# Kurtosis of long rows: the last stage in row form, whole rows for six groups, and dummy transposes before the last sums

## The chip, the cores and the metric

The kernel runs on one core of a Trainium2 chip. The metric is the device time of one execution in microseconds, and the median of several runs is compared. The engines named here are TensorE (PE in the profile, with PEld for its weight loads), VectorE (DVE), ScalarE (ACT), GpSimd (POOL) and SyncE (SP), which issues the DMAs.

## The reference

The input has 1024 rows of 8192 float32 values, 32 MB in all. For each row the excess kurtosis is wanted.

```python
mean = np.mean(x, axis=-1, keepdims=True)
std = np.std(x, axis=-1, keepdims=True)
z = (x - mean) / (std + 1e-8)
return (np.mean(z ** 4, axis=-1) - 3).astype(np.float32)
```

The kernels compute it as n * q / s^2 - 3, where s is the row's sum of squared deviations and q the sum of their squares, that is of the fourth powers.

## The kernel before, in words

**Tiling.** The rows are cut into 18 groups (`GROUPS`). A row is spread over k partitions, so that a group fills 128 partitions with 128/k rows, each partition holding 8192/k columns: k is 8 for the first two groups, 4 for the third and 2 for the other fifteen, which have 4096 columns in each partition. A group's entry gives k, the pieces of columns in which it is loaded (one DMA each), the number of columns whose fourth powers ScalarE takes, and the engine that forms the mean. There are five buffers of 4096 columns (`SLOT_OF`); a group's load is put on SP's queue when the group that held its buffer has been through its fourth powers.

**One group.** The mean comes first. For the early groups (`DVE`) VectorE adds the two halves of each partition with a sum (`added_halves`, L149), and a matmul with a block matrix adds the partitions of a row and divides (L159). For the later groups (`PE`) TensorE transposes the 32 blocks of 128 columns and adds them up in PSUM (`transposed_sums`, L132), VectorE adds the two partitions of a row (`pair_sums`, L138), and a matmul with a column sums up (L168). The last group has `both`: 28 blocks by TensorE and the last piece of 512 columns by VectorE (L164, L165). ScalarE copies the negative mean out of PSUM (`nmu`, L170). Then ScalarE squares the deviations in place, with their sum (`square`, L176). The fourth powers are squares of these: the first columns on ScalarE (L183), the rest on VectorE (L188), each with its sum.

**Order.** The order on each engine is the order of the program text, since the schedule is written out by hand. In step i of the loop stand the mean and the square of group i, the fourth powers of group i-1 on VectorE, the next loads, a piece of work of a finished batch, and the fourth powers of group i on ScalarE. So `pair_sums` of group i stands on VectorE before the fourth powers of group i-1.

**Batches.** The groups' sums are gathered in four batches, and `finish` works on a batch in three steps of the loop: `factor` adds the partitions' sums by a matmul (L204), and forms minus its reciprocal squared on VectorE (L206, L208); `scaled` adds the two engines' fourth powers and multiplies (L215, L216); `result` turns them to rows with a matmul (L226), subtracts 3 (L228), and issues the output DMA on SP (L230).

**The end.** The last group is squared in two halves (L273, L275). VectorE takes the fourth powers of the second half while ScalarE squares the first; then ScalarE takes 1664 columns of the first half and VectorE the other 384. The first-sum matmuls are three (L200 to L202). The last column gets a path of its own: ScalarE's part is scaled on ScalarE (`wa`, L282), VectorE's on VectorE (L284), and two matmuls add them (L226).

Of the kernel before, what the change touches and what calls it, by code (L numbers as in the profile page):

```python
# [7 lines left out]
f32 = mybir.dt.float32  # L8
bf16 = mybir.dt.bfloat16
AO = mybir.AluOpType  # L10
AF = mybir.ActivationFunctionType
P = 128
# [3 lines left out]
GROUPS = [  # L16
    (8, [1024], 0, 'DVE'),
    (8, [1024], 0, 'DVE'),
    (4, [2048], 0, 'DVE'),
    (2, [4096], 1280, 'DVE'),  # L20
    (2, [4096], 768, 'DVE'),
    (2, [4096], 1536, 'DVE'),
    (2, [2304, 1792], 640, 'PE'),
    (2, [2304, 1792], 640, 'PE'),
    (2, [2304, 1792], 640, 'PE'),
    (2, [2304, 1792], 640, 'PE'),
    (2, [2304, 1792], 640, 'PE'),
    (2, [2304, 1792], 640, 'PE'),
    (2, [2304, 1792], 640, 'PE'),
    (2, [1536, 1536, 1024], 512, 'PE'),  # L30
    (2, [1536, 1536, 1024], 512, 'PE'),
    (2, [1536, 1536, 1024], 512, 'PE'),
    (2, [1536, 1536, 1024], 512, 'PE'),
    (2, [1536, 1280, 768, 512], 1664, 'both'),
]

BATCHES = [[0, 1], [2], [3, 4, 5, 6, 7, 8, 9, 10, 11, 12], [13, 14, 15, 16, 17]]
SLOT_W = 4096
SLOT_OF = [0, 1, 2, 3, 0, 1, 2, 3, 4, 0, 1, 2, 3, 4, 0, 1, 2, 3]
HALVES = 2  # L40


@with_exitstack
def kernel(
# [5 lines left out]
    nc = tc.nc  # L50
    n_rows, n_cols = x.shape
# [3 lines left out]
    L = NG - 1  # L55
    KS = [g[0] for g in GROUPS]
# [4 lines left out]
    const = ctx.enter_context(tc.tile_pool(name="const", bufs=1))  # L61
    small = ctx.enter_context(tc.tile_pool(name="small", bufs=4))
    fin = ctx.enter_context(tc.tile_pool(name="fin", bufs=4))
    psum = ctx.enter_context(tc.tile_pool(name="psum", bufs=2, space=bass.MemoryType.PSUM))
    psfin = ctx.enter_context(tc.tile_pool(name="psfin", bufs=1, space=bass.MemoryType.PSUM))
    ctx.enter_context(tc.manual_schedule())

    zeros = const.tile([P, 512], f32, name="zeros")
# [4 lines left out]
    blk = {}  # L73

    def block_matrix(k):
        r = P // k
        b = const.tile([P, P], f32, name=f"blk{k}")
        v = b.rearrange("p (r k) -> p r k", k=k)
        nc.gpsimd.memset(b, neg_inv_n)
        nc.gpsimd.affine_select(  # L80
            out=v, in_=v, pattern=[[-k, r], [0, k]], base=0,
            channel_multiplier=1, compare_op=AO.is_ge, fill=0.0)
        nc.gpsimd.affine_select(  # L83
            out=v, in_=v, pattern=[[k, r], [0, k]], base=k - 1,
            channel_multiplier=-1, compare_op=AO.is_ge, fill=0.0)
        blk[k] = b

    for k in dict.fromkeys(k for k in KS if k > 2):
        block_matrix(k)
    ident = const.tile([P, P], f32, name="ident")  # L90
    nc.gpsimd.memset(ident, 1.0)
    nc.gpsimd.affine_select(
        out=ident, in_=ident, pattern=[[-1, P]], base=0,
        channel_multiplier=1, compare_op=AO.is_equal, fill=0.0)
    negcol = const.tile([P, 1], f32, name="negcol")
    nc.gpsimd.memset(negcol, neg_inv_n)
    block_matrix(2)
    junk = const.tile([P, 2048], bf16, name="junk")

    where = {}
    stats = []
    for b in BATCHES:
        n = len(b) + (b[-1] == L)
        s2, qa, qd = (const.tile([P, n], f32, name=f"{t}_{b[0]}") for t in ("s2", "qa", "qd"))
        if any(GROUPS[i][2] == 0 for i in b):
            nc.gpsimd.memset(qa, 0.0)
        stats.append((s2, qa, qd))
        for j, i in enumerate(b):  # L110
            where[i] = (j, s2, qa, qd)

    slots = [xpool.tile([P, SLOT_W], f32, name=f"xt{s}") for s in sorted(set(SLOT_OF))]
    xts = {}
    nmus = {}

    def load(i):
        k, pieces = GROUPS[i][:2]
        w = n_cols // k
        assert sum(pieces) == w  # L120
        xt = slots[SLOT_OF[i]]
        xts[i] = xt[:, :w]
        src = x[ROWS[i]:ROWS[i + 1], :].rearrange("r (k w) -> (r k) w", k=k)
        c = 0
        for w in pieces:
            nc.sync.dma_start(out=xt[:, c:c + w], in_=src[:, c:c + w])  # L126
            c += w
# [42 lines left out]
        nc.scalar.copy(nmu, mps)  # L170
        nmus[i] = nmu

    def square(i, c0=0, c1=None, extra=0):
        j, s2, qa, qd = where[i]
        t = xts[i][:, c0:c1]
        nc.scalar.activation(out=t, in_=t, func=AF.Square, bias=nmus[i],  # L176
                             accum_out=s2[:, j + extra:j + extra + 1])

    def fourth_act(i, c0, c1):
        j, s2, qa, qd = where[i]  # L180
        if c1 > c0:
            t = xts[i][:, c0:c1]
            nc.scalar.activation(out=t, in_=t, func=AF.Square, accum_out=qa[:, j:j + 1])  # L183

    def fourth_dve(i, c0, c1=None, extra=0):
        j, s2, qa, qd = where[i]
        t = xts[i][:, c0:c1]
        nc.vector.tensor_tensor_reduce(  # L188
            out=t, in0=t, in1=t, scale=1.0, scalar=0.0,
            op0=AO.mult, op1=AO.add, accum_out=qd[:, j + extra:j + extra + 1])  # L190

    def factor(b):
        s2 = stats[BATCHES.index(b)][0]
        n = len(b)
        k = KS[b[0]]
        p2 = psfin.tile([P, n], f32, name="p2")
        if b[-1] == L:
            nc.tensor.matmul(p2[:, :n - 1], lhsT=blk[k], rhs=s2[:, :n - 1], start=True, stop=True)  # L200
            nc.tensor.matmul(p2[:, n - 1:n], lhsT=blk[k], rhs=s2[:, n - 1:n], start=True, stop=False)  # L201
            nc.tensor.matmul(p2[:, n - 1:n], lhsT=blk[k], rhs=s2[:, n:n + 1], start=False, stop=True)  # L202
        else:
            nc.tensor.matmul(p2, lhsT=blk[k], rhs=s2, start=True, stop=True)  # L204
        rec = fin.tile([P, n], f32, name="rec")
        nc.vector.reciprocal(rec, p2)  # L206
        fac = fin.tile([P, n], f32, name="fac")
        nc.vector.scalar_tensor_tensor(  # L208
            out=fac, in0=rec, scalar=-1.0, in1=rec, op0=AO.mult, op1=AO.mult)
        return fac  # L210

    def scaled(b, fac, n):
        s2, qa, qd = stats[BATCHES.index(b)]
        w4 = fin.tile([P, len(b)], f32, name="w4")
        nc.vector.tensor_add(w4[:, :n], qa[:, :n], qd[:, :n])  # L215
        nc.vector.tensor_mul(w4[:, :n], w4[:, :n], fac[:, :n])  # L216
        return w4

    def result(b, terms):
        n = len(b)  # L220
        k = KS[b[0]]
        r = P // k
        sel = blk[k].rearrange("p (r k) -> p r k", k=k)[:, :, 0]
        pk = psfin.tile([n, r], f32, name="pk")
        for j, t in enumerate(terms):
            nc.tensor.matmul(pk, lhsT=t, rhs=sel, start=j == 0, stop=j == len(terms) - 1)  # L226
        kr = fin.tile([n, r], f32, name="kr")
        nc.vector.tensor_scalar_add(kr, pk, -3.0)  # L228
        dst = out[ROWS[b[0]]:ROWS[b[-1] + 1]].rearrange("(g r) -> g r", r=r)
        nc.sync.dma_start(out=dst, in_=kr)  # L230

    def finish(b):
        fac = factor(b)
        yield
        w4 = scaled(b, fac, len(b))
        yield
        result(b, [w4])


    held = {}  # L240
# [2 lines left out]
    def load_next(done):  # L243
        while to_load and held.get(SLOT_OF[to_load[0]], -1) <= done:
            i = to_load.pop(0)
            held[SLOT_OF[i]] = i
            load(i)

    load_next(-1)
    STEPS = [(7, 8, 9), (9, 10, 11), (13, 14, 15)]  # L250
    steps = {}
    for b, ats in zip(BATCHES[:-1], STEPS):
        f = finish(b)
        for at in ats:
            steps.setdefault(at, []).append(f)
    for i in range(L):
        mean(i)
        square(i)
        if i >= 1:
            fourth_dve(i - 1, GROUPS[i - 1][2])  # L260
            load_next(i - 1)
        for f in steps.get(i, ()):
            next(f, None)
        fourth_act(i, 0, GROUPS[i][2])


    k, _, a, _ = GROUPS[L]
    h = n_cols // k // 2
    b = BATCHES[-1]
    n = len(b)  # L270
    s2, qa, qd = stats[-1]
    mean(L)
    square(L, h, 2 * h)  # L273
    fourth_dve(L - 1, GROUPS[L - 1][2])
    square(L, 0, h, extra=1)  # L275
    fourth_dve(L, h, 2 * h)
    fourth_act(L, 0, a)
    fac = factor(b)
    w4 = scaled(b, fac, n - 1)
    wa = fin.tile([P, n], f32, name="wa")  # L280
    nc.gpsimd.memset(wa, 0.0)
    nc.scalar.activation(out=wa[:, n - 1:], in_=qa[:, n - 1:n], func=AF.Copy, scale=fac[:, n - 1:])  # L282
    fourth_dve(L, a, h, extra=1)
    nc.vector.scalar_tensor_tensor(  # L284
        out=w4[:, n - 1:], in0=qd[:, n:], scalar=qd[:, n - 1:n], in1=fac[:, n - 1:],
        op0=AO.add, op1=AO.mult)
    result(b, [wa, w4])


# [28 lines left out]
```

## Time and profile before

| what | value |
|---|---|
| median of five runs | 98.29 us (97.79 to 98.79) |
| the profiled execution's own time | 98.29 us |
| its span | 96.6 us |
| PE busy | 56.7 us (59%), 440 matmuls |
| DVE busy | 76.1 us (79%) |
| ACT busy | 80.0 us (83%) |
| POOL busy | 4.6 us (5%) |
| input loaded | 33.55 MB, 347 GB/s over the span |

The span is the profiled part of the execution; the time of a run holds 1.7 us more around it. Busy shares are averages over a start, a long middle part and an end; on this kernel they have to be read by stretches. A matmul of float32 shows as two instructions, so a pair (x2) is one matmul of the program. In the rows of single instructions the first number is the start in microseconds and the second the duration. An operation with a sum is followed by a short one that reads the accumulator.

### The profile page before, as it was taken

The numbers are of one execution on the slowest core, as the hardware profiler recorded it, in microseconds if no ns is written. First come the engines' busy times: TensorE is split into PE (matmuls) and PEld (weight loads), VectorE is DVE, ScalarE is ACT, GpSimd is POOL, SyncE is SP. The second block draws the span as 40 slices with busy tenths as digits, with TensorE's granted clock in tenths as the row PEclk, the third lists the DMA queues.
The fourth block names the chain that finished last, engine by engine and source line by source line (L and its number), as shares of the span: only waits on it lengthen the run. The fifth ranks groups of instructions, "written<-read, shape, count | busy, mean of one in ns | idle before, by whom it ended". The sixth has DMA issues, their size and how long they took to land.

```text
span 96.6 us, 1268 instructions
## 1 busy us (share of the span) xinstructions
PE 56.7 (59%) x440; PEld 51.2 (53%) x440; DVE 76.1 (79%) x86; ACT 80.0 (83%) x89; POOL 4.6 (5%) x19
## 2 busy tenths in 40 slices
PE   0040202010099797976796979797978797961330
PEld 0040202020099696965695969696967686951310
DVE  2237729899993758989597979698989797999980
ACT  6055440999999899999799999999999899899960
POOL 6830000000000000000000000000000000000000
PEclk9999999999999999999999999999999999996555
DMA  2999999999999999999999999999999999400000
GB/s 44 419 355 451 434 434 428 434 428 357 402 390 410 432 419 438 422 423 422 420 411 431 423 411 413 409 414 411 424 410 421 400 422 405 156 4 0 0 0 4
DMA packets 5226, 33.63 MB, mean 348 GB/s; under 512 B 612, under 2 KB 612, under 8 KB 3812
## 3 DMA queue, kind: packets, MB, share of 16 engines
q1 hardware_dynamic: 5220, 33.56, 84.6%
q8 instruction: 3, 0.05, 0.2%
q14 instruction: 3, 0.02, 0.1%
HBM read 33.55 MB, written 0.00 MB: 347 GB/s over the span
## 4 chain that ended last, share of the span: by engine, by line
DMA 53%; DVE 21%; PE 11%; issue 6%; ACT 6%; SPq 0%; DVEq 0%
DMA xt<-in_x_dram 53%; DVE xt L188 14%; PE tps L132 8%; DVE junk L149 6%; ACT xt L176 5%; PE pk L226 1%; DVE red L138 1%; PE mps L168 1%; PE mps L159 1%; SPq L126 0%; ACT nmu L170 0%; ACT wa L282 0%; DVE qd L188 0%; DVE kr L228 0%; DVE fac L208 0%
## 5 line engine op out<-in xcount | busy, mean ns | idle before, releaser
L176 ACT ACTIVATE xt<-xt,nmu 128x4096 f32<-128x4096 f32 (+2 forms) x19 | 60.4, 3178 | 0.6
L188 DVE CUSTOM_DVE_ANT_0 xt<-xt 128x3456 f32<-128x3456 f32 (+7 forms) x19 | 58.8, 3100 | 1.3 <-ACT nmu L170 1.1
L132 PE MATMUL tps<-ident,xt 128*128 128x128 f32 x380 | 46.6, 280 | 1.4 <-DMA xt<-in_x_dram 1.4
L132 PEld LDWEIGHTS tps<-ident,xt 128*128 128x128 f32 x380 | 43.2, 145 | 3.2 <-DMA xt<-in_x_dram 2.7
L159 PE MATMUL mps<-part,blk 128*128 128x1 f32 x12 | 3.4, 351 | 23.7 <-DVE part L149 23.7
L159 PEld LDWEIGHTS mps<-part,blk 128*128 128x128 f32 x12 | 3.0, 312 | 24.0 <-ACT xt L176 9.1
L149 DVE CUSTOM_DVE_ANT_0 junk<-xt 128x2048 bf16<-128x2048 f32 (+3 forms) x7 | 10.1, 1441 | 6.6 <-DMA xt<-in_x_dram 6.6
L183 ACT ACTIVATE xt<-xt 128x640 f32<-128x640 f32 (+5 forms) x15 | 12.9, 858 | 0.5
L170 ACT COPY nmu<-mps 128x1 f32<-128x1 f32 x18 | 2.7, 152 | 11.5 <-PE mps L159 9.6
L138 DVE TENSOR_REDUCE red<-tps 128x128 f32<-128x256 f32 x12 | 5.1, 424 | 8.8 <-PE tps L132 8.8
L168 PEld LDWEIGHTS mps<-negcol,red 128*128 128x128 f32 x22 | 3.3, 188 | 8.9 <-ACT xt L176 6.5
L168 PE MATMUL mps<-negcol,red 128*128 128x1 f32 x22 | 3.9, 248 | 6.6 <-DVE red L138 4.8
L176 ACT ACTIVATION_READ_ACCUMULATOR xt<-xt,nmu 128x1 f32 x19 | 3.5, 186 | 0.0
L183 ACT ACTIVATION_READ_ACCUMULATOR xt<-xt 128x1 f32 x15 | 2.8, 186 | 0.0
L70 ACT ACT_TABLE_LOAD x1 | 1.3, 1283 | 0.8 <-PEq L302 0.8
L201 PE MATMUL p<-s,blk 128*128 128x1 f32 x2 | 0.6, 363 | 2.2 <-ACT xt L176 2.2
L83 POOL TENSOR_SCALAR_AFFINE_SELECT blk<-blk 128x128 f32<-128x128 f32 x3 | 1.7, 563 | 0.2
L201 PEld LDWEIGHTS p<-s,blk 128*128 128x128 f32 x2 | 0.5, 313 | 2.2 <-ACT xt L176 2.2
L80 POOL TENSOR_SCALAR_AFFINE_SELECT blk<-blk 128x128 f32<-128x128 f32 x3 | 1.7, 553 | 0.2
L188 DVE DVE_READ_ACCUMULATOR2_ANT qd<- 128x1 f32 x19 | 1.6, 83 | 0.0
L202 PE MATMUL p<-s,blk 128*128 128x1 f32 x2 | 0.6, 364 | 1.4 <-ACT xt L176 1.4
L202 PEld LDWEIGHTS p<-s,blk 128*128 128x128 f32 x2 | 0.5, 313 | 1.5 <-ACT xt L176 1.5
(32 smaller groups left out, 13.0 us busy)
## 6 DMA issues: line engine op xcount, KB each, us to landing
xt<-in_x_dram SPq DMA_DIRECT2D x7, 1152.0 KB, 11.7
xt<-in_x_dram SPq DMA_DIRECT2D x9, 768.0 KB, 11.6
xt<-in_x_dram SPq DMA_DIRECT2D x7, 896.0 KB, 13.7
xt<-in_x_dram SPq DMA_DIRECT2D x3, 2048.0 KB, 11.6
xt<-in_x_dram SPq DMA_DIRECT2D x6, 512.0 KB, 11.3
xt<-in_x_dram SPq DMA_DIRECT2D x1, 1024.0 KB, 7.2
xt<-in_x_dram SPq DMA_DIRECT2D x1, 640.0 KB, 11.6
xt<-in_x_dram SPq DMA_DIRECT2D x1, 384.0 KB, 10.6
```

Of the source, the lines that this page charges most:

```text
L70: nc.scalar.activation(out=zeros[:, :1], in_=zeros[:, :1], func=AF.Square)
L80: nc.gpsimd.affine_select(out=v, in_=v, pattern=[[-k, r], [0, k]], base=0, channel_multiplier=1, compare_op=AO.is_ge, fill=0.0)
L83: nc.gpsimd.affine_select(out=v, in_=v, pattern=[[k, r], [0, k]], base=k - 1, channel_multiplier=-1, compare_op=AO.is_ge, fill=0.0)
L132: nc.tensor.matmul(tps, lhsT=xts[i][:, c:c + P], rhs=ident, start=c == 0, stop=c == w - P, is_transpose=True)
L138: nc.vector.tensor_reduce(out=red.rearrange("p (r k) -> p r k", k=2), in_=tps.rearrange("p (r k) -> p r k", k=2).unsqueeze(2).to_broadcast ...
L149: nc.vector.tensor_tensor_reduce(out=junk[:, :h], in0=t[:, :h], in1=t[:, h:], scale=1.0, scalar=0.0, op0=AO.add, op1=AO.add, accum_out=part)
L159: nc.tensor.matmul(mps, lhsT=blk[k], rhs=added_halves(i, 0), start=True, stop=True)
L168: nc.tensor.matmul(mps, lhsT=pair_sums(tps), rhs=negcol, start=True, stop=True)
L170: nc.scalar.copy(nmu, mps)
L176: nc.scalar.activation(out=t, in_=t, func=AF.Square, bias=nmus[i], accum_out=s2[:, j + extra:j + extra + 1])
L183: nc.scalar.activation(out=t, in_=t, func=AF.Square, accum_out=qa[:, j:j + 1])
L188: nc.vector.tensor_tensor_reduce(out=t, in0=t, in1=t, scale=1.0, scalar=0.0, op0=AO.mult, op1=AO.add, accum_out=qd[:, j + extra:j + extra ...
```

## The change

The loads of groups 6 to 8 come in one piece instead of two. ScalarE takes 512 columns of fourth powers instead of 640 in groups 6 to 12, 448 instead of 512 in groups 13 to 15, none in group 16, and 2240 instead of 1664 in group 17. The last group's mean is formed on TensorE alone. It is squared by one instruction; then ScalarE takes columns 0 to 2240 of its fourth powers, and VectorE columns 2816 to 4096 and, after the factor, 2240 to 2816.

The last stage of every batch is in row form: the fourth powers aren't scaled before they are turned to rows. The factor itself is turned to rows by a matmul (`pf`) and copied by ScalarE with a scale (`frow`). ScalarE squares the sums of squares (`sq`); a matmul with a scaled selection matrix (`sel3`, made by GpSimd at the start) adds minus three times that to the fourth powers in PSUM, and the sums of the engines are added by a matmul each. VectorE then multiplies the rows by the factor.

TensorE gets transposes of a tile of zeros into a PSUM tile that nothing reads: 24 behind the matmul of the last mean, ahead of the matmul for the last batch's first sums, and 10 between that one and the matmul for `pf`.

```diff
-    (2, [2304, 1792], 640, 'PE'),
...
-    (2, [1536, 1536, 1024], 512, 'PE'),
...
-    (2, [1536, 1280, 768, 512], 1664, 'both'),
+    (2, [4096], 512, 'PE'),
+    (2, [4096], 512, 'PE'),
+    (2, [4096], 512, 'PE'),
+    (2, [2304, 1792], 512, 'PE'),
...
+    (2, [1536, 1536, 1024], 448, 'PE'),
...
+    (2, [1536, 1536, 1024], 0, 'PE'),
+    (2, [1536, 1280, 768, 512], 2240, 'PE'),
...
+LAST_CUT = 2816
...
+    sel3 = {}
+    for k, b in blk.items():
+        sel3[k] = const.tile([P, P // k], f32, name=f"sel3_{k}")
+        nc.gpsimd.tensor_scalar_mul(
+            sel3[k], b.rearrange("p (r k) -> p r k", k=k)[:, :, 0], -3.0 * n_cols / k)
...
+        quads = [const.tile([P, n], f32, name=f"q{t}_{b[0]}") for t in range(2 + last)]
...
+    def finish(b):
+        s2, quads = stats[b[0]]
         n = len(b)
         k = KS[b[0]]
+        r = P // k
+        sel = blk[k].rearrange("p (r k) -> p r k", k=k)[:, :, 0]
         p2 = psfin.tile([P, n], f32, name="p2")
+        nc.tensor.matmul(p2, lhsT=blk[k], rhs=s2, start=True, stop=True)
         rec = fin.tile([P, n], f32, name="rec")
         nc.vector.reciprocal(rec, p2)
         fac = fin.tile([P, n], f32, name="fac")
         nc.vector.scalar_tensor_tensor(
             out=fac, in0=rec, scalar=-1.0, in1=rec, op0=AO.mult, op1=AO.mult)
-        return fac
-
-    def scaled(b, fac, n):
...
-        nc.vector.tensor_add(w4[:, :n], qa[:, :n], qd[:, :n])
-        nc.vector.tensor_mul(w4[:, :n], w4[:, :n], fac[:, :n])
...
+        yield
+        sq = fin.tile([P, n], f32, name="sq")
+        nc.scalar.activation(out=sq, in_=p2, func=AF.Square)
+        pf = psfin.tile([n, r], f32, name="pf")
+        nc.tensor.matmul(pf, lhsT=fac, rhs=sel, start=True, stop=True)
+        frow = fin.tile([n, r], f32, name="frow")
+        nc.scalar.activation(out=frow, in_=pf, func=AF.Copy, scale=-float(n_cols) / k)
+        yield
         pk = psfin.tile([n, r], f32, name="pk")
-        for j, t in enumerate(terms):
-            nc.tensor.matmul(pk, lhsT=t, rhs=sel, start=j == 0, stop=j == len(terms) - 1)
+        nc.tensor.matmul(pk, lhsT=sq, rhs=sel3[k], start=True, stop=False)
+        for q in quads:
+            nc.tensor.matmul(pk, lhsT=q, rhs=sel, start=False, stop=q is quads[-1])
         kr = fin.tile([n, r], f32, name="kr")
-        nc.vector.tensor_scalar_add(kr, pk, -3.0)
+        nc.vector.tensor_mul(kr, pk, frow)
         dst = out[ROWS[b[0]]:ROWS[b[-1] + 1]].rearrange("(g r) -> g r", r=r)
         nc.sync.dma_start(out=dst, in_=kr)
...
+    idle = psfin.tile([P, P], f32, name="idle")
+
+    def keep_busy(n):
+        for _ in range(n):
+            nc.tensor.matmul(idle, lhsT=zeros[:, :P], rhs=ident, start=True, stop=True,
+                             is_transpose=True)
+
...
+    a = GROUPS[L][2]
+    f = finish(BATCHES[-1])
     mean(L)
-    square(L, h, 2 * h)
+    keep_busy(24)
+    square(L)
     fourth_dve(L - 1, GROUPS[L - 1][2])
-    square(L, 0, h, extra=1)
-    fourth_dve(L, h, 2 * h)
     fourth_act(L, 0, a)
-    fac = factor(b)
-    w4 = scaled(b, fac, n - 1)
-    wa = fin.tile([P, n], f32, name="wa")
-    nc.gpsimd.memset(wa, 0.0)
-    nc.scalar.activation(out=wa[:, n - 1:], in_=qa[:, n - 1:n], func=AF.Copy, scale=fac[:, n - 1:])
-    fourth_dve(L, a, h, extra=1)
-    nc.vector.scalar_tensor_tensor(
-        out=w4[:, n - 1:], in0=qd[:, n:], scalar=qd[:, n - 1:n], in1=fac[:, n - 1:],
-        op0=AO.add, op1=AO.mult)
-    result(b, [wa, w4])
+    fourth_dve(L, LAST_CUT)
+    next(f)
+    keep_busy(10)
+    fourth_dve(L, a, LAST_CUT, second=1)
+    next(f)
+    next(f, None)
```

More of the change, by code (lines that the diff above doesn't have):

```diff
@@ L22 @@
     (2, [4096], 1536, 'DVE'),
-    (2, [2304, 1792], 640, 'PE'),
[L24 to L29, printed above, removed]
-    (2, [1536, 1536, 1024], 512, 'PE'),
-    (2, [1536, 1536, 1024], 512, 'PE'),
-    (2, [1536, 1536, 1024], 512, 'PE'),
-    (2, [1536, 1536, 1024], 512, 'PE'),
-    (2, [1536, 1280, 768, 512], 1664, 'both'),
+    (2, [4096], 512, 'PE'),
+    (2, [4096], 512, 'PE'),
+    (2, [4096], 512, 'PE'),
+    (2, [2304, 1792], 512, 'PE'),
+    (2, [2304, 1792], 512, 'PE'),
+    (2, [2304, 1792], 512, 'PE'),
+    (2, [2304, 1792], 512, 'PE'),
+    (2, [1536, 1536, 1024], 448, 'PE'),
+    (2, [1536, 1536, 1024], 448, 'PE'),
+    (2, [1536, 1536, 1024], 448, 'PE'),
+    (2, [1536, 1536, 1024], 0, 'PE'),
+    (2, [1536, 1280, 768, 512], 2240, 'PE'),
 ]
@@ L38 @@
 SLOT_W = 4096
+LAST_CUT = 2816
 SLOT_OF = [0, 1, 2, 3, 0, 1, 2, 3, 4, 0, 1, 2, 3, 4, 0, 1, 2, 3]
-HALVES = 2
 @with_exitstack
@@ L97 @@
     block_matrix(2)
+    sel3 = {}
[3 more added lines that the diff above has]
+            sel3[k], b.rearrange("p (r k) -> p r k", k=k)[:, :, 0], -3.0 * n_cols / k)
     junk = const.tile([P, 2048], bf16, name="junk")
     where = {}
-    stats = []
+    stats = {}
     for b in BATCHES:
-        n = len(b) + (b[-1] == L)
-        s2, qa, qd = (const.tile([P, n], f32, name=f"{t}_{b[0]}") for t in ("s2", "qa", "qd"))
+        n = len(b)
+        last = b[-1] == L
+        s2 = const.tile([P, n], f32, name=f"s2_{b[0]}")
+        quads = [const.tile([P, n], f32, name=f"q{t}_{b[0]}") for t in range(2 + last)]
         if any(GROUPS[i][2] == 0 for i in b):
-            nc.gpsimd.memset(qa, 0.0)
-        stats.append((s2, qa, qd))
+            nc.gpsimd.memset(quads[0], 0.0)
+        if last:
+            nc.gpsimd.memset(quads[2], 0.0)
+        stats[b[0]] = (s2, quads)
         for j, i in enumerate(b):
-            where[i] = (j, s2, qa, qd)
+            where[i] = (j, s2, quads)
     slots = [xpool.tile([P, SLOT_W], f32, name=f"xt{s}") for s in sorted(set(SLOT_OF))]
@@ L171, in mean, with square, fourth_dve @@
         nmus[i] = nmu
[L173 to L177, printed above, removed]
+    def square(i):
+        j, s2, _ = where[i]
+        nc.scalar.activation(out=xts[i], in_=xts[i], func=AF.Square, bias=nmus[i],
+                             accum_out=s2[:, j:j + 1])
     def fourth_act(i, c0, c1):
-        j, s2, qa, qd = where[i]
+        j, _, quads = where[i]
         if c1 > c0:
             t = xts[i][:, c0:c1]
-            nc.scalar.activation(out=t, in_=t, func=AF.Square, accum_out=qa[:, j:j + 1])
-    def fourth_dve(i, c0, c1=None, extra=0):
-        j, s2, qa, qd = where[i]
+            nc.scalar.activation(out=t, in_=t, func=AF.Square, accum_out=quads[0][:, j:j + 1])
+    def fourth_dve(i, c0, c1=None, second=0):
+        j, _, quads = where[i]
         t = xts[i][:, c0:c1]
@@ L189, in fourth_dve @@
             out=t, in0=t, in1=t, scale=1.0, scalar=0.0,
-            op0=AO.mult, op1=AO.add, accum_out=qd[:, j + extra:j + extra + 1])
-    def factor(b):
-        s2 = stats[BATCHES.index(b)][0]
+            op0=AO.mult, op1=AO.add, accum_out=quads[1 + second][:, j:j + 1])
+    def finish(b):
+        s2, quads = stats[b[0]]
         n = len(b)
         k = KS[b[0]]
+        r = P // k
+        sel = blk[k].rearrange("p (r k) -> p r k", k=k)[:, :, 0]
         p2 = psfin.tile([P, n], f32, name="p2")
[L199 to L204, printed above, removed]
+        nc.tensor.matmul(p2, lhsT=blk[k], rhs=s2, start=True, stop=True)
         rec = fin.tile([P, n], f32, name="rec")
@@ L209, in factor @@
             out=fac, in0=rec, scalar=-1.0, in1=rec, op0=AO.mult, op1=AO.mult)
-        return fac
-    def scaled(b, fac, n):
-        s2, qa, qd = stats[BATCHES.index(b)]
-        w4 = fin.tile([P, len(b)], f32, name="w4")
-        nc.vector.tensor_add(w4[:, :n], qa[:, :n], qd[:, :n])
-        nc.vector.tensor_mul(w4[:, :n], w4[:, :n], fac[:, :n])
[L217 to L223, printed above, removed]
+        yield
[6 more added lines that the diff above has]
+        yield
         pk = psfin.tile([n, r], f32, name="pk")
-        for j, t in enumerate(terms):
-            nc.tensor.matmul(pk, lhsT=t, rhs=sel, start=j == 0, stop=j == len(terms) - 1)
+        nc.tensor.matmul(pk, lhsT=sq, rhs=sel3[k], start=True, stop=False)
+        for q in quads:
+            nc.tensor.matmul(pk, lhsT=q, rhs=sel, start=False, stop=q is quads[-1])
         kr = fin.tile([n, r], f32, name="kr")
-        nc.vector.tensor_scalar_add(kr, pk, -3.0)
+        nc.vector.tensor_mul(kr, pk, frow)
         dst = out[ROWS[b[0]]:ROWS[b[-1] + 1]].rearrange("(g r) -> g r", r=r)
         nc.sync.dma_start(out=dst, in_=kr)
-    def finish(b):
-        fac = factor(b)
[L234 to L237, printed above, removed]
     held = {}
@@ L264 @@
         fourth_act(i, 0, GROUPS[i][2])
[L267 to L271, printed above, removed]
+    a = GROUPS[L][2]
+    f = finish(BATCHES[-1])
     mean(L)
-    square(L, h, 2 * h)
+    keep_busy(24)
+    square(L)
     fourth_dve(L - 1, GROUPS[L - 1][2])
-    square(L, 0, h, extra=1)
-    fourth_dve(L, h, 2 * h)
     fourth_act(L, 0, a)
-    fac = factor(b)
-    w4 = scaled(b, fac, n - 1)
-    wa = fin.tile([P, n], f32, name="wa")
-    nc.gpsimd.memset(wa, 0.0)
-    nc.scalar.activation(out=wa[:, n - 1:], in_=qa[:, n - 1:n], func=AF.Copy, scale=fac[:, n - 1:])
-    fourth_dve(L, a, h, extra=1)
-    nc.vector.scalar_tensor_tensor(
-        out=w4[:, n - 1:], in0=qd[:, n:], scalar=qd[:, n - 1:n], in1=fac[:, n - 1:],
-        op0=AO.add, op1=AO.mult)
-    result(b, [wa, w4])
+    fourth_dve(L, LAST_CUT)
[4 more added lines that the diff above has]
+    next(f, None)
 _INS = ['x']
```

## The prediction

> **What bounds the kernel now.** The page is read first for the row of DMA shares and the granted TensorE clock, in 40 slices of 2.4 us.
>
> ```profile
> PEclk9999999999999999999999999999999999996555
> DMA  2999999999999999999999999999999999400000
> ```
>
> The DMA engines are full from the second slice to the 34th; then twelve microseconds follow in which nothing is loaded. So there are two stages with different limits: a body in which work on VectorE, ScalarE and TensorE costs nothing while it keeps up with the loads, and a tail after the last data. The clock falls to one half in the tail. The sums by stretches show how the loading ends (columns: stretch, its length, clock, DMA share, GB/s):
>
> ```profile
> 81.00:82.00 1.00, 1.00 0.99 393
> 82.00:83.00 1.00, 1.00 0.70 268
> 83.00:84.00 1.00, 1.00 0.31 119
> 84.00:85.00 1.00, 1.00 0.12 44
> ```
>
> It ends raggedly: most of the 16 engines are done at 82.5, the last at about 85. Then the timeline of each engine, from the last group's mean on. ScalarE (start, duration, line, operation):
>
> ```profile
> 82.59 3.74 ACT L176 ACTIVATE xt<-xt,nmu 128x4096 f32<-128x4096 f32 x1
> 86.22 0.20 ACT L176 ACTIVATION_READ_ACCUMULATOR xt<-xt,nmu 128x1 f32 x1
> 86.45 0.63 ACT L183 ACTIVATE xt<-xt 128x512 f32<-128x512 f32 x1
> ...
> 91.42 1.59 ACT L183 ACTIVATE xt<-xt 128x1664 f32<-128x1664 f32 x1
> 92.92 0.19 ACT L183 ACTIVATION_READ_ACCUMULATOR xt<-xt 128x1 f32 x1
> 93.19 0.30 ACT L282 ACTIVATE wa<-qa,fac 128x1 f32<-128x1 f32 x1
> ```
>
> ScalarE is dense from the square of group 16 to 93.49. VectorE:
>
> ```profile
> 86.45 3.89 DVE L188 CUSTOM_DVE_ANT_0 xt<-xt 128x3584 f32<-128x3584 f32 x1
> ...
> 93.06 0.55 DVE L188 CUSTOM_DVE_ANT_0 xt<-xt 128x384 f32<-128x384 f32 x1
> 93.53 0.08 DVE L188 DVE_READ_ACCUMULATOR2_ANT qd<- 128x1 f32 x1
> 93.65 0.22 DVE L284 SCALAR_TENSOR_TENSOR w<-qd,fac 128x1 f32<-128x1 f32 x1
> 94.34 0.21 DVE L228 TENSOR_SCALAR kr<-pk 5x64 f32<-5x64 f32 x1 [0.47 <-PE pk L226]
> ```
>
> It is dense too. TensorE:
>
> ```profile
> 82.24 3.45 PE L132 MATMUL tps<-ident,xt 128*128 128x128 f32 x28
> 86.50 0.35 PE L164 MATMUL mps<-negcol,red 128*128 128x1 f32 x2 [0.81 <-ACT xt L176]
> 86.72 0.36 PE L165 MATMUL mps<-part,blk 128*128 128x1 f32 x2
> ...
> 93.53 0.38 PE L226 MATMUL pk<-blk,wa 128*5 128x64 f32 x2 [1.50 <-ACT wa L282]
> 93.92 0.37 PE L226 MATMUL pk<-blk,w 128*5 128x64 f32 x2
> ```
>
> Everything after the first of the two L226 pairs is serial: w at 93.87, second pair, `kr` at 94.34, output DMA, end at 96.6. The sum below is therefore the new start of `kr`; the 2.03 us after `kr` and the 1.69 us between span (96.6) and profiled time (98.29) stay. That time happens to equal the median, 98.29; the five runs spread from 97.79 to 98.79, so a difference under about 1% can't be told from none.
>
> **Body: whole loads for groups 6 to 8.** The trace's packet records show 611 ns for a row of 4096 in one packet, and for the two pieces 347 + 272 ns (22 to 40 us) or 351 + 274 ns later. An engine carries 8 of the 128 rows, so three groups save 24 x 8 to 14 ns = 0.19 to 0.34 us of a full queue; I take 0.26, and keep 0 as the other end. The price: transposes of these groups start at the landing of the whole group, not of 2304 columns. Group 6 landed in full at 28.75, while TensorE had started at 26.92 and ended at 32.03. Starting at 28.8 with 32 transposes, 20 at the early pace of 6 to 7 per us and 12 at 12 per us, it ends at 32.9, or at 33.7 if the slow pace lasts: 0.9 to 1.7 us late. This lag goes through `red` to ScalarE and, as `red` stands before the fourth powers of group 5, to the release of that slot, so to group 10's load (issued at 36.7 instead of 35.3). What covers it: at 36.7 groups 8 (landing 38.9) and 9 (landing 43 to 45) are still queued. ScalarE and VectorE must win the lag back: ScalarE's period was 4.75 us where nothing held it (square of group 7 at 37.97, of 8 at 42.72), with 512 instead of 640 columns 0.11 less, against 5.0 us per group of loads (33.5 MB at 420 GB/s). So 0.36 us are won per group; the lag is gone by group 12 or 13. `sq` and `frow` add about 0.4 us to ScalarE once per batch; the last such time is in group 14, leaving two groups with 448 or no columns to win that back. VectorE's 3584 or 3648 columns take 3.88 to 3.95 us, with `red` under 4.4 of 5.0. Price 0; if the cover failed, up to the whole lag.
>
> The other body edits: VectorE loses two small operations per batch (0.16 us each), ScalarE takes theirs; POOL's three small multiplications stand behind the matrix for pairs, done at 5.6 us and first wanted at 16, so 10 us cover them, and the output DMAs keep their places on SP between the loads. Nothing.
>
> **Last mean.** Now 32 transposes: 28 ended at 85.69, four more at 3.92/32 = 0.12 us give 86.18 (the last piece landed at 85.25 at the latest). `red` starts at 86.20, not 85.94. But the added halves and the pair at L165 go: group 16 took 0.96 us from the start of `red` (81.44) to `nmu` (82.40). So `nmu` 87.16 (was 87.11), square 0.19 later at 87.35 (was 87.31). With the loads' 0.26: **87.09**. That group 16 no longer has fourth powers on ScalarE gains nothing here: ScalarE waits for the mean.
>
> **One square, ScalarE.** Start to end of the accumulator read: 82.59 to 86.42, 3.83 us, so 90.92 (was 91.39 with two halves). Fourth powers of 2240 columns: 1664 took 1.69 to the end of the read (91.42 to 93.11), 576 more at (1590 - 630)/1152 = 0.83 ns are 0.48, so 90.95 + 2.17 = 93.12. Then `sq`, 128x5 from PSUM: between the 0.15 of an `nmu` copy and the 0.30 of `wa`; 0.2 by the nearer. It may start 0.06 before the read ends, as `nmu` did at 87.11. End **93.28**.
>
> **VectorE.** Group 16, 4096 columns: from about 86.28 in 4.42 us (3.88 plus 512 at 1.04 ns) to 90.70, just before the square ends. The 1280 columns from 90.95 take 1.49, the reciprocal follows at 92.37, `fac` ends 0.39 later at 92.76, the 576 columns (0.55 + 192 at 1.04 ns = 0.75) start 0.31 after the reciprocal and end at **93.43**.
>
> **TensorE at the end.** The queue is `sq`, ScalarE's fourth powers, and the two columns of VectorE: four pairs where two stood, without `wa` and `w`. At full clock pairs follow each other by 0.22 (86.50, 86.72, 86.94) and one of 10x64 lasted 0.28. From 93.32: 3 x 0.22 + 0.28 = 0.94, end 94.26, `kr` at **94.28** against 94.34. VectorE's last column is ready 0.5 us before its pair's turn (93.98), so ScalarE's `sq` ends the chain. At half clock pairs last 0.38 and their spacing lies between 0.22 and 0.38, so 0.1 to 0.6 us more; I take 0.3.
>
> **Dummies.** 24 at 0.12 are 2.9 us, from 87 to 90, in front of the first-sum matmul that can't run before 90.95: covered by 1 us; at the slow pace of 0.15 (27 to 30 us) still covered. Ten more end at 92.5, or, with the slow 0.59 us matmul ahead, near 93.0, where `fac` was ready at 92.76: 0.25 us for `frow`, which has 0.6 us until `kr`. What they buy is the clock. Before, it fell at 87.86, after a stretch in which TensorE was mostly busy, so a partly idle stretch can end it. Transposes alone do raise the pace; the stretches of L132 count them:
>
> ```profile
> 29.00:30.00 1.00, 1.00 (x7) 1.00 (x6) 1.00 1.00 406
> 30.00:31.00 1.00, 1.00 (x12) 1.00 (x11) 1.00 0.95 399
> ```
>
> Seven per us become twelve with nothing but transposes running. [...]
>
> **Sum:** ScalarE starts its last fourth powers 0.47 earlier (-0.26 loads, +0.04 mean, -0.25 one square with its gap) and needs 0.48 more for them, but `sq` ends 0.21 before `wa` did, as it waits for nothing and is shorter. From there to `kr` it is 1.00 instead of 0.85. -0.21 + 0.15 = -0.06: 98.2.
>
> **Rivals.**
> 1. *The clock isn't held* (the change doesn't do what it says). For: half clock from 87.86 although TensorE had been 60% busy in the 3.4 us before; the gap between the 24th dummy (90) and the sums (90.95). Against: the pace row. +0.3: 98.5; without the loads' gain 98.8, slower than before.
> 2. *A ragged end that moves, earlier.* The page has three instruction fetches (q8); their packets lasted 1.1 us each on one engine, and after the first, at 41.3, one engine landed 2.4 us behind the first instead of 1.1. The changed program has other instruction counts, so fetches may fall on engines that have slack. Then the landing at 83.68 that started the last 16 transposes comes 1.1 us earlier: 97.1. Against: nothing in the change aims at it.
> 3. *The lag reaches the end: slower.* The 0.9 to 1.7 us of groups 6 to 8 stay if ScalarE's period isn't below the loads' 5.0 us; the place is the square of group 17, the price, less than the middle since the first groups win some back, 1.1: 99.3. It decides from a period over 4.9, against 4.64 worked out. A fetch that falls on the engine already last costs the same 1.1 us.
>
> **Numbers.** Forecast 0.50; clock lost 0.22 (98.5 to 98.8); earlier landing 0.15 (97.1); lag or later landing 0.13 (99.3). The range takes in both outer cases and the unknown spacing: 97.0 to 99.3. Faster by over 1% (below 97.3) is most of the third case and a little of the first, 0.16; slower by over 1% (above 99.3) part of the last and the upper end of the second, 0.14; the rest 0.70.
>
> **What would show it.** Clock 1.0 in the rows from 88 to 93, or 0.5; the last mean at about 87.1; one L176-like square of 3.74 us; VectorE's last column ready before TensorE comes to its pair; four pairs of 0.22; squares of groups 13 to 16 no later than before. Wrong if the last landing differs by over 0.5 us, if `kr` waits for VectorE, or if ScalarE is still late at group 14.

## The result and the profile after

The changed kernel is slower: the ratio to the kernel before is 1.0076, 95% interval 1.0054 to 1.0098, which is some 0.75 us. This ratio leaves out runs that lie more than 1.5% above the fastest of their kernel, 22 of the changed kernel's 43; with all runs the medians are 99.22 and 98.10 us, 1.1 us apart, as the changed kernel's single runs spread wider (97.75 to 100.36). The forecast was 98.2, a shade faster than the 98.29 that it started from. The profiled execution of the changed kernel took 98.76 us with a span of 97.0. The six whole groups of the title are 3 to 8; of these, 3 to 5 came in one piece before as well.

The page's slices after, clock and DMA share:

```profile
PEclk9999999999999999999999999999999999999999
DMA  2999999999999999999999999999999999100000
```

The clock no longer falls in the tail, and the loads end as early as before. So neither explains the loss. The page's chain of what ended last, by engine, does:

```profile
PE 36%; ACT 28%; DMA 21%; DVE 8%; issue 2%; SPq 1%; ACTq 0%; DVEq 0%
```

Before, DMA held 53% of that chain. After, the chain leaves the loads for good at group 6. The same chain in order of time (start, duration, engine, tile and line):

```profile
27.74 6.45 PE tps L141 x32
...
53.79 0.38 PE mps L177 x2
54.18 0.21 PE pf L219 x2
54.38 3.66 PE tps L141 x32
58.04 0.02 issue
58.06 0.43 DVE red L147
...
58.63 0.35 PE mps L177 x2
58.99 0.15 PE pk L224 x2
59.14 0.23 PE pk L226 x4
59.37 3.66 PE tps L141 x32
```

Group 6's 32 transposes take 6.45 us, against 5.11 before: they start at the slow pace of 0.21 us apart, and go on at 0.11 once the clock has risen. The clock row above can't show that, since the trace's clock record begins with the first rise (at 33.35 us here, at 29.84 before), and what lies ahead of it is printed as full speed.

From group 8 to group 12 the body then runs at the pace of a loop over two engines: a mean's matmul, the transposes of the next group behind it, the pair sums on VectorE, the next mean. The round from 54.38 to 59.37 is 3.66 us of transposes, 0.59 for the pair sums with the gaps beside them, 0.36 for the mean's matmul, and 0.38 for the lines at 58.99 and 59.14. These two lines and that at 54.18 are finishing steps of the second batch; those of the first stand in the rounds before. Without such steps a round is 4.61 us, just under the 4.64 of ScalarE.

The two profiles don't begin alike: the first square of 4096 columns (group 3) starts at 17.14 before and at 16.39 after. The squares of groups 3, 6 and 17 before, then those of groups 3 and 6 after:

```profile
17.14 3.71 ACT L176 ACTIVATE xt<-xt,nmu 128x4096 f32<-128x4096 f32 x1
...
33.22 3.73 ACT L176 ACTIVATE xt<-xt,nmu 128x4096 f32<-128x4096 f32 x1
...
87.31 2.00 ACT L176 ACTIVATE xt<-xt,nmu 128x2048 f32<-128x2048 f32 x1
...
16.39 3.71 ACT L184 ACTIVATE xt<-xt,nmu 128x4096 f32<-128x4096 f32 x1
...
35.36 3.72 ACT L184 ACTIVATE xt<-xt,nmu 128x4096 f32<-128x4096 f32 x1
```

What comes later is best measured from that point, up to which both kernels do the same:

| start, from the square of group 3 | before | after | difference |
|---|---|---|---|
| square of group 6 | 16.08 | 18.97 | +2.89 |
| square of group 8 | 25.58 | 28.25 | +2.67 |
| square of group 12 | 45.93 | 47.76 | +1.83 |
| square of group 17 | 70.17 | 71.26 | +1.09 |
| last `kr` | 77.20 | 78.11 | +0.91 |

A lag of 2.9 us arises at group 6, melts slowly, and 1.1 us of it reaches the last group. The tail then wins 0.2 back. (The two times differ by 0.47 us: 0.91 at `kr`, less 0.75 of earlier start, plus 0.31 from the start of `kr` to the end, a stretch that takes 2.2 to 3.0 us in the profiles here.) The tail in the timeline after:

```profile
87.46 0.16 ACT L179 COPY nmu<-mps 128x1 f32<-128x1 f32 x1 [0.52 <-PE mps L177]
87.65 3.72 ACT L184 ACTIVATE xt<-xt,nmu 128x4096 f32<-128x4096 f32 x1
...
91.49 2.08 ACT L191 ACTIVATE xt<-xt 128x2240 f32<-128x2240 f32 x1
...
93.56 0.16 ACT L217 ACTIVATE sq<-p 128x5 f32<-128x5 f32 x1
...
93.77 0.28 PE L224 MATMUL pk<-sel,sq 128*5 128x64 f32 x2
...
93.88 0.51 PE L226 MATMUL pk<-blk,q 128*5 128x64 f32 x6
93.93 0.08 DVE L196 DVE_READ_ACCUMULATOR2_ANT q<- 128x1 f32 x1
94.50 0.21 DVE L228 TENSOR_TENSOR kr<-pk,frow 5x64 f32<-5x64 f32 x1 [0.48 <-PE pk L226]
```

From the last square to `kr` it is 6.85 us, against 7.03 before: the four pairs are through at 94.4, 0.62 us after the first of them starts.

### The profile page after: what moved, and what is told of

Read it like the earlier page. It is cut to its first block, busy times and chain, and to the rows that moved or that the text cites. A ratio compares the mean times of both kernels' runs of the same rounds, so it can differ in the third digit from the quotient of the medians.

```text
span 97.0 us, 1368 instructions
## 1 busy us (share of the span) xinstructions
PE 61.2 (63%) x496; PEld 56.7 (58%) x496; DVE 75.8 (78%) x75; ACT 78.7 (81%) x92; POOL 5.9 (6%) x23
## 4 chain that ended last, share of the span: by engine, by line
PE 36%; ACT 28%; DMA 21%; DVE 8%; issue 2%; SPq 1%; ACTq 0%; DVEq 0%
PE tps L141 29%; ACT xt L184 24%; DMA xt<-in_x_dram 21%; PE mps L177 4%; ACT xt L191 3%; DVE red L147 3%; DVE junk L158 2%; DVE xt L196 2%; SPq L135 1%; PE pk L226 1%; ACT nmu L179 1%; PE pk L224 1%; PE p L209 1%; PE pf L219 0%; DVE kr L228 0%
## 5 line engine op out<-in xcount | busy, mean ns | idle before, releaser
L196 DVE CUSTOM_DVE_ANT_0 xt<-xt 128x3584 f32<-128x3584 f32 (+9 forms) x19 | 60.0, 3158 | 1.3 <-ACT nmu L179 1.1
L141 PE MATMUL tps<-ident,xt 128*128 128x128 f32 x384 | 47.1, 284 | 1.4 <-DMA xt<-in_x_dram 1.4
L141 PEld LDWEIGHTS tps<-ident,xt 128*128 128x128 f32 x384 | 44.9, 148 | 2.1 <-DMA xt<-in_x_dram 1.5
L158 DVE CUSTOM_DVE_ANT_0 junk<-xt 128x2048 bf16<-128x2048 f32 (+2 forms) x6 | 9.7, 1617 | 5.8 <-DMA xt<-in_x_dram 5.8
L191 ACT ACTIVATE xt<-xt 128x512 f32<-128x512 f32 (+5 forms) x14 | 11.8, 843 | 0.4
L177 PE MATMUL mps<-negcol,red 128*128 128x1 f32 x24 | 4.4, 251 | 6.9 <-DVE red L147 4.5
L248 PE MATMUL idle<-ident,zeros 128*128 128x128 f32 x34 | 4.1, 275 | 0.0
L248 PEld LDWEIGHTS idle<-ident,zeros 128*128 128x128 f32 x34 | 3.8, 145 | 0.0
L209 PE MATMUL p<-s,blk 128*128 128x2 f32 (+3 forms) x8 | 1.5, 258 | 1.4 <-ACT xt L184 1.4
L196 DVE DVE_READ_ACCUMULATOR2_ANT q<- 128x1 f32 x19 | 1.6, 83 | 0.0
```

What stands on the lines that cost most here:

```text
L141: nc.tensor.matmul(tps, lhsT=xts[i][:, c:c + P], rhs=ident, start=c == 0, stop=c == w - P, is_transpose=True)
L158: nc.vector.tensor_tensor_reduce(out=junk[:, :h], in0=t[:, :h], in1=t[:, h:], scale=1.0, scalar=0.0, op0=AO.add, op1=AO.add, accum_out=part)
L177: nc.tensor.matmul(mps, lhsT=pair_sums(tps), rhs=negcol, start=True, stop=True)
L196: nc.vector.tensor_tensor_reduce(out=t, in0=t, in1=t, scale=1.0, scalar=0.0, op0=AO.mult, op1=AO.add, accum_out=quads[1 + second][:, j:j + 1])
L248: nc.tensor.matmul(idle, lhsT=zeros[:, :P], rhs=ident, start=True, stop=True, is_transpose=True)
```

## The experiments

Two theories stood at first. LAG: the whole loads make TensorE begin group 6 late and slow, and the lag isn't won back. ROW FORM: the new last stage costs time in the body by itself. All ratios are to the kernel before, from five rounds, reckoned as the one above; beside some of them stand the medians of all runs.

**Groups 6 to 8 in two pieces again**, all else as changed.

```diff
-    (2, [4096], 512, 'PE'),
+    (2, [2304, 1792], 512, 'PE'),
```

> The changed kernel with groups 6 to 8 loaded in two pieces again, all else as changed. Theory LAG (the whole loads make TensorE start group 6 late and at the slow pace, and the lag is never won back): the square of group 6 starts near 33.2 us instead of 35.4, the last mean comes near 87.1, and as the tail from the last mean to kr is 0.2 us shorter than before, the ratio to the kernel before is 0.995 to 1.000. Theory ROW FORM (the added matmuls and ScalarE operations of the new last stage in the body cost the time): the ratio stays near 1.0076.

Measured: 0.9981 (0.9954 to 1.0009). As LAG has it. In the profile the square of group 6 stands 16.15 us after that of group 3, where it stood before (16.08). That one execution can't serve for the end: it took 99.68 us, the clock having fallen to half from 44.1 to 47.5 us behind a wait of 1.1 us for a load, while all other runs lay between 97.6 and 98.3. Behind that wait it lies as far back as the changed kernel does: 1.97 us at group 9 (there 1.98), and 0.90 at `kr` (there 0.91). So a lag of that size stays in part wherever it comes from.

**The kernel before with groups 6 to 8 whole**, and nothing else.

```diff
-    (2, [2304, 1792], 640, 'PE'),
+    (2, [4096], 640, 'PE'),
```

> The kernel before with groups 6 to 8 loaded whole, nothing else. Theory LAG: the ratio is 1.007 to 1.012, since its ScalarE share of 640 columns wins the lag back more slowly than the changed kernel. Theory ROW FORM: 0.997 to 1.000, the whole loads being cheaper on the queue by 0.26 us.

Measured: 1.0077 (1.0030 to 1.0123); the medians of all runs are 99.40 and 98.11 us. The whole loads alone cost what the whole change does. In its profile the square of group 6 stands 19.05 us after that of group 3, that of group 17 at 70.97, and the squares between follow each other by 4.75 us: here ScalarE's period with 640 columns, not TensorE's loop, holds the lag.

**No dummies.** Both calls are left out.

```diff
-    keep_busy(24)
...
-    keep_busy(10)
```

> The changed kernel without any dummy transposes. If they hold the clock and that is worth what the prediction took (0.3 us), the granted clock falls to 0.5 near 88 to 91 us and the ratio to the kernel before is about 1.011. If the dummies buy nothing, 1.0076; if they cost, less.

Measured: 1.0153 (1.0095 to 1.0211). The trace's clock record falls at 91.0, and the tail's matmuls show it:

```profile
91.86 0.59 PE L209 MATMUL p<-s,blk 128*128 128x5 f32 x2 [4.08 <-ACT xt L184]
...
94.11 0.38 PE L224 MATMUL pk<-sel,sq 128*5 128x64 f32 x2
...
94.28 0.85 PE L226 MATMUL pk<-blk,q 128*5 128x64 f32 x6
```

The pairs take 0.85 where they took 0.51, and from the last square to `kr` it is 7.24 us instead of 6.85: 0.39 us for the clock. The ratios differ by more, 0.75 us, but the interval of this one reaches 0.6 us to either side; the medians of all runs, 99.68 and 99.22, are 0.46 us apart.

**Warming TensorE ahead of group 6.** The changed kernel with dummies behind earlier means.

```diff
     for i in range(L):
         mean(i)
+        keep_busy({4: 20, 5: 10}.get(i, 0))
```

> The changed kernel with 20 further dummy transposes behind the mean of group 4 and 10 behind that of group 5, so that TensorE has been busy before group 6 lands. Theory LAG: group 6's 32 transposes take 3.7 us instead of 6.4, the lag at group 6 falls from 2.1 us to about 0, and the ratio to the kernel before is 0.990 to 0.998. Theory ROW FORM: no change, 1.0076. If dummies don't raise the clock, the transposes of group 6 keep 6.4 us.

Measured: 1.0037 (0.9990 to 1.0084), but the single runs lie in two clusters, 98.2 to 99.1 and 100.4 to 100.9, and the medians of all runs are 100.46 and 98.11 us. The expected 0.990 to 0.998 was missed. In the profile the 30 dummies ran at the slow pace (20 in 4.51 us), the clock rose only at 31.3, and the second ten held group 6 back to 29.35. Why the runs fall into two clusters isn't settled.

**Only group 6 in two pieces, and only group 6 whole.** Is it the first group or each? The first diff is for group 6 in two pieces, the second for groups 7 and 8.

```diff
-    (2, [4096], 512, 'PE'),
+    (2, [2304, 1792], 512, 'PE'),
     (2, [4096], 512, 'PE'),
     (2, [4096], 512, 'PE'),
```

```diff
     (2, [4096], 512, 'PE'),
-    (2, [4096], 512, 'PE'),
-    (2, [4096], 512, 'PE'),
+    (2, [2304, 1792], 512, 'PE'),
+    (2, [2304, 1792], 512, 'PE'),
```

> The changed kernel with only group 6 in two pieces again; groups 7 and 8 stay whole. Theory FIRST GROUP (only the first transposed group matters, as TensorE is slow there and then lies behind the landing of groups 7 and 8 anyway): as the kernel with all three in pieces, ratio 0.995 to 1.000. Theory EVERY GROUP (each whole load adds its delay): about 1.004, between the changed kernel and the one with three groups in pieces.

> The changed kernel with only group 6 whole; groups 7 and 8 in two pieces again. FIRST GROUP: 1.006 to 1.009, as the changed kernel, with a wide spread of single runs. EVERY GROUP: about 1.003.

Measured: 1.0021 (0.9988 to 1.0055) with only group 6 in pieces, 1.0093 (1.0050 to 1.0137) with only group 6 whole (medians of all runs 99.29 and 98.05 us). The first result lies just above the expected range, and the 1.004 of EVERY GROUP lies inside its interval too; the second decides, as its interval excludes 1.003. The whole loss comes with group 6. Groups 7 and 8 whole cost little: in the first profile the square of group 6 is 0.8 us late against the kernel before, that of group 7 0.9, that of group 12 still 0.3, and that of group 17 is 0.4 early.

**Without finishing the first two batches.** The loop leaves out their steps.

```diff
-    for b, ats in zip(BATCHES[:-1], STEPS):
+    for b, ats in list(zip(BATCHES[:-1], STEPS))[2:]:
```

> The changed kernel without finishing its first two batches (the results of groups 0 to 2, the first 64 rows, are left out): their nine row-form and sum matmuls, their small operations on ScalarE and VectorE and two output DMAs are gone. Theory LOOP (while the lag lasts, the body runs at the pace of TensorE's loop mean, transposes, pair sums, mean, and the matmuls of the finishing steps stand inside it): the squares of groups 9 to 12 follow each other by 4.64 us instead of 4.74 to 5.03, the lag is gone earlier, ratio 1.000 to 1.004. If the finishing is covered, as the prediction had it: 1.0076.

Measured: 1.0017 (0.9979 to 1.0054). In the profile group 6 is even later than in the changed kernel (19.15 us after the square of group 3), yet all squares from group 6 to group 14 follow each other by 4.64 us, where the changed kernel had 4.74, 5.03, 4.81 and 4.93 between groups 8 and 12. The square of group 17 comes at 70.38, 0.9 us sooner.

**The same finishing, in another place.** To separate the place from the work, the two batches are finished in steps 2 to 6, where TensorE is mostly idle; whole loads stay.

```diff
-    STEPS = [(7, 8, 9), (9, 10, 11), (13, 14, 15)]
+    STEPS = [(2, 3, 4), (4, 5, 6), (13, 14, 15)]
```

> The changed kernel, whole loads and all, with the first two batches finished in steps 2 to 6 instead of 7 to 11. Theory LOOP: as without that finishing, the squares of groups 8 to 12 follow each other by 4.64 us, ratio 1.000 to 1.004. If it was the work left out there and not its place in TensorE's loop that made the difference: 1.0076.

Measured: 0.9994 (0.9955 to 1.0033). The medians of all runs, 98.50 and 98.09 us, give 1.004, where the changed kernel's give 1.011. The chain in order of time:

```profile
50.51 3.81 ACT xt L184 x2
...
55.15 3.82 ACT xt L184 x2
...
59.79 3.83 ACT xt L184 x2
```

ScalarE is in the chain now, at 4.64 us per group, and the lag melts: 2.9 us at group 6 (36.31 less 17.33, against 16.08), 0.3 at group 17, 0.1 at `kr` (94.67). Nothing was taken out; three batches are finished with the same instructions. So both parts were needed for the changed kernel's loss: the lag, and the finishing steps in the loop that should have won it back. The profiles put a figure to it. From group 8 to group 17 the changed kernel, and each of the six variants that keep its steps and lag by over 1 us at group 8, win back 1.4 to 1.6 us. With whole loads and the first two batches finished early, or not at all, it is 2.6.

**A longer warming**, with whole loads and the change's own steps.

```diff
+        keep_busy({3: 24, 4: 26, 5: 6}.get(i, 0))
```

> The changed kernel with 24 further dummy transposes behind the mean of group 3, 26 behind that of group 4 and 6 behind that of group 5. Twenty and ten had not raised the clock in time, with a gap in TensorE's work at 26 us, and the ten delayed the start of group 6 by 1.6 us. [...]

Measured: 1.0055 (1.0017 to 1.0093), above the 0.993 to 1.000 that LAG gave for a TensorE at full pace before group 6 lands; the medians of all runs are 98.94 and 98.05 us. TensorE's timeline in its profile:

```profile
16.98 4.13 PE L248 MATMUL idle<-ident,zeros 128*128 128x128 f32 x24
...
21.67 3.04 PE L248 MATMUL idle<-ident,zeros 128*128 128x128 f32 x26
...
28.69 3.71 PE L141 MATMUL tps<-ident,xt 128*128 128x128 f32 x32 [0.94 <-DMA xt<-in_x_dram]
...
34.54 3.71 PE L141 MATMUL tps<-ident,xt 128*128 128x128 f32 x32 [1.18 <-DMA xt<-in_x_dram]
```

In this execution it worked: group 6's transposes take 3.71 us and the lag at group 6 is 0.2. Group 7 then waits 1.18 us for its own whole load and is 1.3 late, which is won back; at group 17 the kernel is 0.2 us ahead of the one before, at `kr` 0.4. But this run had a mean clock of 1.0; the others with 1.0 or 0.98 took 97.9 to 98.8, and those with 0.961 to 0.965 took 98.9 to 100.2. Where the clock was lower in these was not seen in a profile.

**Towards a better version.** Two pieces with 34 and 12 dummies, that with the early finishing as well, and the plain two-piece kernel once more beside them.

```diff
-    keep_busy(24)
+    keep_busy(34)
...
-    keep_busy(10)
+    keep_busy(12)
```

> Groups 6 to 8 in two pieces and 34 and 12 dummies, the finishing steps where the change has them. If the clock still falls in the tail of some runs with 24 and 10 (it did in one profile, at 92.8 us, where kr then waited 0.4 us longer), single runs lie closer together and the ratio is 0.1 to 0.2% below the same kernel with 24 and 10; if the dummies already held it, equal.

> The changed kernel with groups 6 to 8 in two pieces, the first two batches finished in steps 2 to 6 (when TensorE is mostly idle) instead of 7 to 11, and 34 and 12 dummies instead of 24 and 10, so that no gap is left before the last sums. If the loads bound the body and the tail is 0.2 us shorter than before, or 0.4 less where the clock would have fallen: ratio to the kernel before 0.993 to 0.998. If one of the moved steps holds TensorE up at groups 2 to 6: over 1.000.

> The same kernel as the one with groups 6 to 8 in two pieces, for a narrower interval beside its variants: 0.996 to 1.000.

Measured: 0.9979 (0.9955 to 1.0003), 0.9999 (0.9975 to 1.0024) and 1.0019 (0.9992 to 1.0045). The second and the third lie above what was expected. All three beat the changed kernel; none beats the kernel before beyond its interval. The two-piece kernel came out at 0.9981 and 1.0019 on two occasions, so 0.3% is what such a comparison can tell here. With 34 and 12 dummies the mean clock was at least 0.995 in every run; with 24 and 10 it was 0.981 to 0.982 in four of twelve.

## Why the prediction was wrong

**The step that failed is the cover of the lag** under "whole loads for groups 6 to 8", in two places. The outcome is the third rival, which had a chance of 0.13 and a price of 1.1 us; 0.75 was measured, or 1.1 by the medians of all runs. The rival was to decide by a period of over 4.9 us on ScalarE. From group 9 to group 12 the period was 4.92, but another engine's loop made it.

First the size: 0.9 to 1.7 us were priced, 2.9 came (2.1 by the profiles' own clocks). That the transposes start later was foreseen, and they do, by 1.57 us. The pace was not. The slow pace was read off counts of instructions in stretches, 6 to 7 per us or 0.15 us each, but slow transposes start 0.21 us apart: an instruction that crosses the border of a stretch is counted in both. (By an estimate from that pace, 24 x 0.21, the 24 dummies would take 5.0 us too, and not be covered.) And the slow pace was taken to end after 20 transposes. Before, it had ended after 14; in the changed kernel's profile it lasted for 27 of the 32. The lag of 2.9 us is the 1.57 of the start and 1.32 by which the 32 transposes took longer, 6.43 us against 5.11.

This second part is not the whole load's doing alone. In the profiles without dummies ahead of group 6, the clock rises 2.9 to 6.1 us after its first transpose, with one piece or two, and its 32 transposes take 5.11 to 6.66 us. It rose early in the profile of the kernel before, and late in that of the two-piece kernel with 34 and 12 dummies; group 6 in these two profiles:

```profile
26.92 5.11 PE L132 MATMUL tps<-ident,xt 128*128 128x128 f32 x32
...
27.18 6.66 PE L141 MATMUL tps<-ident,xt 128*128 128x128 f32 x32
```

The second of them lags by 1.55 us at group 6, and is level at group 17. A lag within the prediction's price was won back, then; one of 2.9 was not.

Second the recovery: 0.36 us per group, by ScalarE's period of 4.64 against 5.0 of the loads. The 4.64 is right, as the early finishing shows. The 5.0 was too much: the squares before stand 4.92 us apart on average from group 6 to group 17, and only 4.75 from 6 to 8, so that even at 4.64, in the run that doesn't finish the first two batches, only 0.26 us per group were won from group 6 to group 17. In the changed kernel it was 0.16, as ScalarE was not the engine that set the pace from group 8 to group 12. The loop from mean to mean over TensorE and VectorE is 3.7 us of transposes, some 0.6 for the pair sums with their gaps, and 0.4 for the mean; and every matmul between a mean and the next transposes lengthens it. The prediction looked at the finishing steps' cost on ScalarE and VectorE, and never put their matmuls on TensorE into a loop. In the profile before, TensorE's transposes waited for loads three times, 1.4 us in all; in the changed kernel's the only such wait stands ahead of group 6.

**The gain of 0.26 us in the queue** can't be seen: the chain doesn't pass through the loads any more, and the last load lands 68.1 us after the square of group 3 in both profiles.

**The tail** was right in sign. Predicted were 7.19 us from the last square to `kr`, measured 6.85; the pairs start 0.11 to 0.12 us apart, closer than the 0.22 us of pairs with 128 columns of weights that the prediction took. `sq` ended the chain, as worked out, though VectorE's last column (94.01) came only about 0.1 us before its pair's turn, not 0.5.

**The dummies** did what they were said to: clock 1.0, and 0.39 us longer without them, where 0.3 was taken. That float32 transposes alone raise the clock, as the prediction read off the pace row, shows in the longer warming too: with little but dummy transposes running, the clock record rises at 19.7 us, the first 24 of them take 4.13 us and the next 26 take 3.04, and group 6's transposes take 3.71 us instead of 6.43.

## What to carry to other kernels

A step is covered only while the engine that covers it stays the bound: after a shift, look for the loop that then sets the pace, over all engines, and count every small instruction queued inside it. Where a kernel gains only a few per cent on its loads, a lag of 3 us lives for ten groups (here 2.89 us at group 6 and still 1.09 at group 17); work that can be done where the lagging engine is idle belongs there. A coarser load saved nothing that could be seen here, and took away the head start of the first consumer, where that consumer starts slowly (here 0.21 us per transpose, against 0.11 later). And a lag between two single profiles holds the luck of both: read it from several.

## What the hardware showed that was not expected

The clock rises and falls at other times in each run. In the profile before, the trace's clock record rises at 29.84 us and falls at 87.87; without dummies it rises at 32.99 and falls at 91.02: 58.03 us apart in both. In the changed kernel's profile it rises at 33.35 and doesn't fall before the end. With the time of the rise moves the time at which TensorE speeds up in group 6, whose 32 transposes take 5.11, 5.74 and 6.43 us in these three. What sets the time of the rise was not shown. The six runs without dummies give an estimate of what a late one costs where nothing covers it. The higher the mean clock here, the later it fell in the tail, if it is one half from the fall to the end in all six as in the profiled one; and the later it rose, if rise and fall are 58.03 us apart in all six as well. For the other five no trace shows either.

| mean clock | 0.962 | 0.964 | 0.965 | 0.966 | 0.967 | 0.968 |
|---|---|---|---|---|---|---|
| us | 98.96 | 99.21 | 99.53 | 99.84 | 99.96 | 100.10 |

Worked out from clock and span (0.962 and 97.2 us, 0.968 and 98.4), the fall moves from about 89.8 to 92.1 us, so by this estimate 2.3 us of later speed cost 1.1 us of time. It fits the pace: 2.3 us hold 11 transposes at 0.21 us, and at 0.11 they take 1.1 us less. The kernel before shows no such order among its runs: beside the last experiments a mean clock of 0.956 came with 97.42 and 98.27 us, and the highest, 0.971, with 97.86. That the first piece's head start covers a late rise there fits the two-piece profile above that rose late and was level at group 17, but no profile of the kernel before with a late rise was taken.
